# Named steps in one interleaved table, GpSimd's work moved, and a column-tiled expert gather in a one-core hybrid diffusion layer

## The chip, the cores and the metric

The kernel runs on one core of a Trainium2 chip. The metric is the device time of one execution in microseconds (us), smaller is better. Three runs of the kernel before took 646.40, 644.19 and 645.77 us; the median is 645.77.

The core has five instruction queues, each of which runs its instructions in order: TensorE (PE in the profile, its weight loads as PEld), VectorE (DVE), ScalarE (ACT), GpSimd (POOL) and SyncE (SP, which here only issues loads). An instruction that waits holds up everything behind it on its own queue.

## The reference

One trunk layer on 256 latent tokens and 256 context tokens of width 1024, in fp32. Cut to what matters:

```python
mod_x = silu(c) @ w_ada + b_ada              # six vectors of 1024: sh1, sc1, g1, sh2, sc2, g2
ux = (rms_norm(x, norm1) * (1 + sc1) + sh1) @ w_in       # and uc for the context tokens
fx, qx, kx, vx, bx, cx, hx = split_in(ux)                # kc, vc from uc
attn = na_latent(qx / 8, kx, vx, kc, vc, rpb)   # 8 heads; neighbours in the grid + all context keys, one softmax
conv = bx * short_conv(cx * hx, w_conv)         # width 3 over the positions
mixed = concat([fourier_mix(fx) @ w_fourier, attn, conv]) @ w_out
x = x + g1 * mixed
t = rms_norm(x, norm2) * (1 + sc2) + sh2
# router: best of 4 groups, then the best two of its 8 experts, softmax weights
for e in range(32):
    y += combine[:, e] * ((silu(t @ w_gate[e]) * (t @ w_up[e])) @ w_down[e])
out = rms_norm(x + g2 * y)
```

## The kernel before

**Streaming.** All large weights go through ten slabs of 16 KB per partition (2.1 MB each); an eleventh is added when the front's scratch memory is given up. `queue` fixes the order of the loads. `pump()` (L108) issues loads from SyncE while a slab is free; `drop()` (L138) gives one back. A load waits on SyncE until the last reader of the slab's old contents is done, and the loads behind it wait too. Some slabs hold no weights: `c` (context input), `g` (small operands, the convolution's data), `a` (attention bias, queries), `u`, `uh`, `ul` (the modulated input and its two exact parts), `kv`, `f` (Fourier tables), `cat` (the mixed heads).

**The front** (all before the experts) is straight-line code; its order in the source is the order on every engine. `normalise` and `transposed` bring x into feature-major form, `first_rows` and `first_columns` make the first shift and scale, `modulate` applies them, `band` (L242) makes the attention bias. `project` (L350) multiplies with both operands split in two exact parts, three products per block; `ahead` (L337) makes the parts of a weight block, the high one by ScalarE, the low one by VectorE. Order of the projections: Fourier and outer gate beside keys, then values, queries, convolution. `sums` (L308) makes the other modulation vectors on VectorE, one piece of a weight slab at a time.

**Attention** (from L460) works on two heads at a time: `scores` for both query halves (four products), bias and running minimum on VectorE, exponentials on ScalarE, division by the sum on VectorE (L481), `ptrans` transposes the probabilities, `pv` (L491) multiplies with the values. `mix` (L506) adds a row block of the output projection. GpSimd multiplies w_out by the first gate (`fold`, L501, in two calls) and does the convolution (L546 to L552). Then `x1` (L637) adds the residual, `logits` (L652) and `route` (L657) are the router.

**Experts.** Each of 32 experts has 32 places. `group(g)` (L748) gathers the tokens of four experts by products with one-hot rows, 16 products of 128 columns, and makes the weighted one-hot rows for the way back. `hidden(e)` (L785) makes the hidden layer, in four column tiles of 32; `project_down(e)` (L809) the output, and `scatter(g)` (L778) adds four experts' rows to their tokens in PSUM.

## Time and profile before

| | us |
|---|---|
| median of three runs | 645.77 |
| profiled execution, first to last instruction (span) | 641.5 |
| TensorE busy, share of the span | 476.4 (74%) |
| VectorE busy | 226.8 (35%) |
| ScalarE busy | 144.8 (23%) |
| GpSimd busy | 44.5 (7%) |
| data moved | 246.12 MB, 384 GB/s on average |
| share of DMA on the chain that ended last | 62% |

The profile is one execution. A row of a timeline reads: start, duration, engine, source line, operation, output tile, input tiles, shape and count, and in brackets how long the engine had been idle and what released it. Rows of a stage table give each engine's busy time in a stretch, the granted TensorE clock as a share of full speed, the mean busy share of the 16 DMA engines and the rate. TensorE issues a product before the one ahead has left the array, so durations overlap; start to start is the pace. Tiles have the names of the program: `b` and `m` are PSUM banks, `ws` a split weight block, `acc` the probabilities (and the partial sums before), `gu` and `dn` expert weights.

### The profile page before, as it was taken

To read this page: it belongs to the slowest core of one execution; us is meant where nothing else is said; L and a number is where in the kernel's file an instruction comes from. 1 tells how busy PE (TensorE), PEld (TensorE's weight loads), DVE (VectorE), ACT (ScalarE), POOL (GpSimd) and SP (SyncE) were. 2 spreads that over 40 slices of the span, in tenths; PEclk is the share of its full clock that TensorE was granted. 3 is DMA by queue.
4 is the path that set the end of the run, shared out by engine and by line. 5 is a ranking of instruction groups with operands and counts; after the bars stand their busy time and mean duration, and the time that the engine had idled before them with its cause. 6 is when DMAs were issued, how large, how long until landed. Compare 5 with 4: busy or idle time off the path is not lost.

```text
span 641.5 us, 11030 instructions
## 1 busy us (share of the span) xinstructions
PE 476.4 (74%) x4775; PEld 307.9 (48%) x4775; DVE 226.8 (35%) x525; ACT 144.8 (23%) x322; POOL 44.5 (7%) x44
## 2 busy tenths in 40 slices
PE   3999999887987887585567555855946585568785
PEld 3787898544775454253235222632523253235442
DVE  4767877999744222021011000211210021012323
ACT  4524234454642111011001000110100011003003
POOL 1000000894000000000000000000000000000000
PEclk9999999888997999898779778797888888789798
DMA  9999579953797999999999999999999999999992
GB/s 351 422 419 360 222 277 372 428 230 147 295 399 297 429 426 424 426 426 427 426 427 423 425 430 423 422 425 426 424 428 426 425 429 424 426 426 428 423 381 102
DMA packets 21220, 246.12 MB, mean 384 GB/s; under 512 B 2214, under 2 KB 3242, under 8 KB 6956
## 3 DMA queue, kind: packets, MB, share of 16 engines
q1 hardware_dynamic: 21016, 245.08, 91.9%
q8 instruction: 39, 0.64, 0.4%
q10 hardware_dynamic: 148, 0.27, 0.1%
q14 instruction: 17, 0.14, 0.1%
HBM read 244.28 MB, written 1.05 MB: 382 GB/s over the span
## 4 chain that ended last, share of the span: by engine, by line
DMA 62%; PE 26%; DVE 8%; ACT 1%; issue 1%; SPq 1%; DVEq 0%; ACTq 0%
DMA gu<-in_w_gu 41%; DMA dn<-in_w_dn 18%; PE b L360 11%; PE m L792 3%; DMA ada<-in_w_ada 3%; PE b L517 2%; DVE f L317 2%; DVE acc L481 2%; PE m L761 1%; PE m L814 1%; DVE ws L344 1%; PE b L261 1%; PE b L488 1%; PE m L951 1%; DVE acc L475 1%
## 5 line engine op out<-in xcount | busy, mean ns | idle before, releaser
L792 PE MATMUL m<-gu,xg 128*32 128x256 f32 x2048 | 139.9, 425 | 63.8 <-DMA gu<-in_w_gu 60.2
L792 PEld LDWEIGHTS m<-gu,xg 128*32 128x32 f32 x2048 | 72.9, 120 | 125.5 <-DMA gu<-in_w_gu 43.3
L814 PE MATMUL m<-dn,ht 128*32 128x256 f32 x992 | 74.3, 450 | 26.7 <-DMA dn<-in_w_dn 19.6
L802 DVE TENSOR_TENSOR hh<-m,sg 128x128 f32<-128x128 f32 x32 | 9.3, 291 | 182.0 <-ACT sg L800 182.0
L814 PEld LDWEIGHTS m<-dn,ht 128*32 128x32 f32 x992 | 38.8, 125 | 50.5 <-issue 38.5
L822 DVE COPY yg<-m 32x256 f32<-32x256 f32 x56 | 23.4, 418 | 99.1 <-PE m L814 86.8
L822 ACT COPY yg<-m 32x256 f32<-32x256 f32 x56 | 20.4, 364 | 142.8 <-DVE yg L822 142.8
L360 PE MATMUL b<-uh,ws 128*128 128x256 f32 (+1 forms) x224 | 52.1, 317 | 0.1
L800 ACT ACTIVATE sg<-m 128x128 f32<-128x128 f32 x32 | 8.9, 278 | 161.2 <-PE m L792 161.2
L360 PEld LDWEIGHTS b<-uh,ws 128*128 128x128 f32 x224 | 37.0, 188 | 4.7 <-issue 1.2
L360 PE MATMUL b<-ul,ws 128*128 128x256 f32 (+1 forms) x112 | 35.1, 313 | 0.0
L769 POOL TENSOR_TENSOR sw<-st,cmb 128x256 f32<-128x256 f32 x8 | 5.8, 725 | 418.4 <-DVE st L694 293.4
L783 PE MATMUL m<-yg,sl 128*128 128x512 f32 x56 | 27.7, 639 | 6.4 <-ACT yg L822 6.4
L761 PEld LDWEIGHTS m<-sr,xs 128*128 128x128 f32 x224 | 28.7, 208 | 7.7 <-PEq L887 4.8
L761 PE MATMUL m<-sr,xs 128*128 128x128 f32 x224 | 28.9, 292 | 4.0 <-DVE sr L754 4.0
L344 DVE TENSOR_TENSOR ws<-in,ws 128x1024 fp32r<-128x1024 f32 x20 | 24.4, 1221 | 14.9 <-ACT ws L343 14.8
L767 DVE TENSOR_SCALAR xg<-m,a,sh 128x128 f32<-128x128 f32 x32 | 13.1, 410 | 45.4 <-PE m L761 36.9
L804 PE MATMUL m<-ident,hh 128*128 128x128 f32 x32 | 10.9, 340 | 23.7 <-DVE hh L802 23.7
L765 ACT ACTIVATE xg<-m,sh,a 128x128 f32<-128x128 f32 x32 | 14.6, 458 | 59.4 <-DVE xg L767 59.4
L360 PE MATMUL b<-ws,uh 128*128 128x512 f32 (+1 forms) x96 | 25.9, 354 | 1.9 <-ACT uh L300 1.9
L517 PE MATMUL b<-ws,cat 128*128 128x512 f32 x96 | 24.3, 402 | 0.0
L804 PEld LDWEIGHTS m<-ident,hh 128*128 128x128 f32 x32 | 4.6, 143 | 40.9 <-DVE hh L802 40.8
(236 smaller groups left out, 574.4 us busy)
## 6 DMA issues: line engine op xcount, KB each, us to landing
gu<-in_w_gu SPq DMA_DIRECT2D x63, 2048.0 KB, 39.2
dn<-in_w_dn SPq DMA_DIRECT2D x31, 2048.0 KB, 39.1
ada<-in_w_ada SPq DMA_DIRECT2D x12, 2048.0 KB, 9.0
in<-in_w_in SPq DMA_DIRECT2D x3, 2048.0 KB, 11.3
in<-in_w_in SPq DMA_DIRECT2D x8, 512.0 KB, 17.2
out<-in_w_out SPq DMA_DIRECT2D x2, 2048.0 KB, 10.8
gu<-in_w_gu SPq DMA_DIRECT2D x4, 512.0 KB, 32.5
dn<-in_w_dn SPq DMA_DIRECT2D x3, 512.0 KB, 11.5
```

The costliest lines, as they stand in the source:

```text
L317: DVE.scalar_tensor_tensor(a, w, scx[:, j:j + 1], a, op0=OP.mult, op1=OP.add)
L344: DVE.tensor_tensor(ws[:, 1], src, ws[:, 0].bitcast(F32), OP.subtract)
L360: PE.matmul(po, wv if wst else uv, uv if wst else wv, start=(j == 0 and m == 0 and n == 0), stop=(j == NJ - 1 and m == len(parts) - 1 and ...
L517: PE.matmul(yo[t, h], cat[:, a, MIX[n], blk(t)], ws[:, b, h, :], start=(first and k == 0), stop=(last and k == 2))
L761: PE.matmul(pg[:, j, :], xs[:, t, jj * P:(jj + 1) * P], sr[:, t], start=(t == 0), stop=(t == 1))
L765: ACT.activation(xg[:, jj, :], pg[:, j, :], AF.Identity, bias=sh2[:, 0, jj:jj + 1], scale=a2[:, 0, jj:jj + 1])
L767: DVE.tensor_scalar(xg[:, jj, :], pg[:, j, :], a2[:, 0, jj:jj + 1], sh2[:, 0, jj:jj + 1], op0=OP.mult, op1=OP.add)
L783: PE.matmul(yp[2 * t + h], sl[:, t, :], yg[:, blk(h, 512)], start=(g == 0), stop=(g == NE // 4 - 2))
L792: PE.matmul(pg[32 * q:32 * q + 32], xg[:, j, CAP * i:CAP * (i + 1)], wgu[j // 4][:, :, j % 4, q * P:(q + 1) * P], start=(j == 0), stop=(j ...
L804: PE.transpose(pt, hh, ident)
L814: PE.matmul(pd[32 * q:32 * q + 32, :], ht[:, 32 * k:32 * k + 32], wdn[:, q, k, :], start=(k == 0), stop=(k == 3))
L822: (ACT.copy if q % 2 else DVE.tensor_copy)(dst, src)
```

## The change

**Named steps.** The front is cut into small functions by name; a table, `STEPS`, lists 375 of them, and they run in that order. A line of it:

```
m0t10 z3_ y3_ s4 cl0 cw1 m0t01 m4t11 hi23 s5 X4 cm1 m1t01 m4t00 cl1 E4 p1 X5 dg g3 R4 E5 lo23 e9 ph1 m2t00 S4 m2t11 pl1 m4t10 R5
```

`s5` is the pair of score products of unit 5 (two heads, one half of the queries), `X`, `E`, `R`, `S`, `t` and `y.._`/`z.._` are its bias, exponentials, division, transposes and copies, `p1` the product with the values, `m4t10` three products of row block 4 of w_out for token half 1 and output half 0, `hi`/`lo` the parts of a weight block, `e9` a piece of a sum, `d..` a slab given back.

**Work that moves.** GpSimd no longer touches w_out nor the convolution. The gate is applied by VectorE to the projected rows (`x`); the convolution is VectorE's; half of the divisions, and three of four modulations, are ScalarE's; VectorE copies half of the transposed probabilities. The load order changes, and `spare` is gone. The routing of both token halves runs after both halves' logits.

**Experts.** `group` makes only the one-hot rows; `gather(e)` gathers one expert's tokens in four column tiles and is called inside `hidden` of the expert before. The softmax weights and the rows for the way back (`weights`, `weighted`) come after the first expert's `hidden`.

```diff
-    queue += [("in", 3, w_in[3])] + first[0:2] + [("in", 2, w_in[2]), first[2], ("in", 4, w_in[4]), first[3]]
-    queue += [("small", 0, small_b)] + [("ada2", t, w_ada[8 + t]) for t in range(2)]
-    queue += [("out", 0, w_out[0])] + [("ada2", t, w_ada[8 + t]) for t in range(2, 4)] + [("out", 1, w_out[1])]
+    queue += first[0:2] + [("in", 3, w_in[3]), ("small", 0, small_b), first[2], ("in", 2, w_in[2]), first[3]]
+    queue += [("ada2", 0, w_ada[8]), ("in", 4, w_in[4]), ("ada2", 1, w_ada[9]), ("out", 0, w_out[0]), ("out", 1, w_out[1])]
+    queue += [("g2", 0, b_g2)] + [("ada2", t, w_ada[8 + t]) for t in range(2, 4)]
...
-    def fold(i):
-        for c in range(4):
-            w = loaded["out", i][:, blk(c, D)]
-            POOL.tensor_tensor(w, w, g1b, OP.mult)
...
+    @each("cw{}", range(2))
+    def _(m):
+        z = ct[:, m, :]
+        DVE.tensor_scalar(z, cp[:, m, 0:SEQ], wc[:, m:m + 1], None, op0=OP.mult)
+        for i in (1, 2):
+            DVE.scalar_tensor_tensor(z, cp[:, m, i:SEQ + i], wc[:, 2 * i + m:2 * i + m + 1], z, op0=OP.mult, op1=OP.add)
+        DVE.tensor_tensor(z, z, gbt[:, m, :], OP.mult)
...
+    @each("R{}", range(8))
+    def _(u):
+        mx, p = mxs[:, 2 * (u % 4):2 * (u % 4) + 2, :], pb[u % 2][0]
+        DVE.reciprocal(mx[:, :, 3:4], mx[:, :, 2:3])
+        DVE.tensor_scalar(p, p, mx[:, 0, 3:4], None, op0=OP.mult)
+
+    @each("S{}", range(8))
+    def _(u):
+        p = pb[u % 2][1]
+        ACT.activation(p, p, AF.Copy, scale=mxs[:, 2 * (u % 4) + 1, 3:4])
...
+    @each("x{}{}", range(2), range(2))
+    def _(t, h):
+        hs = blk(h, 512)
+        DVE.tensor_tensor(junk[:, hs], held["yo", t, h], g1b[:, hs], OP.mult)
+        DVE.tensor_tensor(xs[:, t, hs], junk[:, hs], xs[:, t, hs], OP.add)
...
+    run("g8 b0 b1 Ba0 B0 Ba1")
+    normalise(xs)
+    run("B1")
+    transposed()
+    run(STEPS)
...
+    def gather(e):
+
+        g, i = divmod(e, 4)
+        xg, sr = state[g][0], state[g][3]
+        pg = mbank((P, 256))
+        for t in range(2):
+            for q in range(4):
+                PE.matmul(pg[32 * q:32 * q + 32, :], sr[:, t, i, :], xs[:, t, blk(q, 256)], start=(t == 0), stop=(t == 1))
+        gt = mo.tile([P, 256], F32, name="gt", tag="sw")
+        (DVE.tensor_copy if e % 2 else ACT.copy)(gt, pg)
+        pt = mbank((P, 2, 4, CAP))
+        for c in range(2):
+            PE.transpose(pt[:, c], gt[:, blk(c)], ident)
+        dst = xg[:, i].rearrange("p (q c) n -> p c q n", c=2)
+        for v, op, src in ((a2, OP.mult, pt), (sh2, OP.add, dst)):
+            w = v.rearrange("p o (q c) -> p (o c) q", c=2)[..., None].to_broadcast([P, 2, 4, CAP])
+            DVE.tensor_tensor(dst, src, w, op)
...
     def expert(e):
         g, i = divmod(e, 4)
-        ht = hidden(e)
+        ht = hidden(e, {NJ - 1: (e + 1,)} if i < 3 else {}, gather)
+        if i == 0:
+            if g == 0:
+                weights()
+            weighted(g)
         project_down(e, ht, state[g][2], i)
```

TensorE's order in attention before, from the first transposes on (L488 transposes of probabilities, L467 scores, L517 output projection, L496 products with the values, L329 a sum over partitions, L596 the router's bias):

```order
L488 MATMUL b<-ident,acc 128x128 x16
L467 MATMUL b<-kv,a 128x512 x4
L517 MATMUL b<-ws,cat 128x512 x12
L496 MATMUL b<-f,kv 64x256 x8
L329 MATMUL b<-f,ones 32x256 x4
L517 MATMUL b<-ws,cat 128x512 x12
L488 MATMUL b<-ident,acc 128x128 x16
L467 MATMUL b<-kv,a 128x512 x4
L517 MATMUL b<-ws,cat 128x512 x12
L596 MATMUL b<-sa,sh_1111 1x40 x8
```

The same engine after, in the middle of attention (L699 transposes, L664 scores, L722 output projection, L709 products with the values, L470 half of the second gate):

```order
L722 MATMUL b<-ws,cat 128x512 x3
L709 MATMUL b<-f,kv 64x256 x8
L722 MATMUL b<-ws,cat 128x512 x3
L699 MATMUL b<-ident,acc 128x128 x8
L722 MATMUL b<-ws,cat 128x512 x3
L664 MATMUL b<-kv,a 128x512 x2
L722 MATMUL b<-ws,cat 128x512 x6
L664 MATMUL b<-kv,a 128x512 x2
L722 MATMUL b<-ws,cat 128x512 x6
L709 MATMUL b<-f,kv 64x256 x8
L470 MATMUL b<-ada_3_1300,scx 32x256 x16
L722 MATMUL b<-ws,cat 128x512 x9
```

Scores come two at a time instead of four, transposes eight instead of sixteen, and three to nine products of the output projection stand between them.

GpSimd's order before, from its claim of the slab `kv` on (L504 is `fold`, L548 to L552 the convolution):

```order
L92 COPY kv<-cst 128x1
L92 CAST cat<-cst 128x1
L504 TENSOR_TENSOR out_1004<-out_1004,g 128x1024 x4
L548 TENSOR_SCALAR g<-g,sa 128x256
L550 TENSOR_SCALAR g<-g,sa 128x256
L551 TENSOR_TENSOR g<-g 128x256
```

and after, from the last of its constants on (L882 is the weighted one-hot rows):

```order
L207 TENSOR_SCALAR iota_r<-iota_e 128x32
L209 TENSOR_SCALAR trib<-acc 128x128
L108 COPY kv<-cst 128x1
L108 CAST cat<-cst 128x1
L882 TENSOR_TENSOR sw<-st,cmb 128x256 x4
```

Between the claim of `cat` and the experts nothing is left on GpSimd.

TensorE's order where the experts begin, before (L761 gather, L772 transposes of the weighted rows, L792 hidden layer, L804 its transpose, L814 down product):

```order
L761 MATMUL m<-fsr,xs 128x128 x16
L772 MATMUL m<-ident,sw 128x128 x2
L792 MATMUL m<-gu_0_1153,xg 32x256 x16
L792 MATMUL m<-gu_0_1277,xg 32x256 x16
L804 MATMUL m<-ident,hh 128x128
L814 MATMUL m<-dn_1279,ht 32x256 x16
```

and after (L897 and L902 gather, L922 hidden layer, L934 its transpose, L885 the weighted rows, L944 down product):

```order
L897 MATMUL m<-xs,fsr 32x256 x8
L902 MATMUL m<-ident,gt 128x128 x2
L922 MATMUL m<-gu_0_1302,xg 32x256 x16
L922 MATMUL m<-gu_0_1412,xg 32x256 x16
L897 MATMUL m<-xs,fsr 32x256 x8
L902 MATMUL m<-ident,gt 128x128 x2
L934 MATMUL m<-ident,hh 128x128
L885 MATMUL m<-ident,sw 128x128 x2
L944 MATMUL m<-dn_1431,ht 32x256 x16
```

One expert's share of the gather stands ahead of the first expert; the next expert's share and the weighted rows stand between its hidden and its down product. (The order counts an fp32 product once; the trace shows two instructions for it.)

## Rows read from the trace of the kernel before

**Rows 1.** The page: the span, and the chain that ended last by engine.

```profile
span 641.5 us, 11030 instructions
...
DMA 62%; PE 26%; DVE 8%; ACT 1%; issue 1%; SPq 1%; DVEq 0%; ACTq 0%
```

**Rows 2.** Stage table: PE, PEld, DVE, ACT, POOL busy, clock, DMA share, GB/s.

```profile
17.20:112.40 95.20, 94.88 (x777) 80.24 (x777) 72.96 (x118) 37.69 (x60) 0.30 (x1) 1.00 0.86 344
112.40:150.00 37.60, 28.85 (x165) 18.61 (x165) 35.77 (x68) 17.54 (x39) 34.51 (x21) 0.89 0.68 280
150.00:190.80 40.80, 39.42 (x242) 28.75 (x240) 27.43 (x80) 23.38 (x50) 1.01 (x1) 0.97 0.80 317
190.80:205.60 14.80, 10.29 (x104) 8.23 (x103) 7.38 (x39) 5.41 (x13) 0.62 (x1) 0.77 0.72 282
205.60:627.00 421.40, 290.61 (x3352) 163.08 (x3352) 69.91 (x182) 47.55 (x131) 6.24 (x11) 0.88 1.00 423
```

**Rows 3.** Timeline of SyncE's load issues, 187 to 204 us.

```profile
187.38 3.84 SPq L136 DMA_DIRECT2D gu<-in_w_gu  x2
203.64 0.33 SPq L136 DMA_DIRECT2D dn<-in_w_dn  x1
```

**Rows 4.** Timeline of PE: first projection product, last logits, gather, expert 0.

```profile
17.22 0.39 PE L360 MATMUL b<-ws,uh 128*128 128x256 f32 x1 [1.92 <-ACT uh L300]
...
188.84 1.98 PE L655 MATMUL b<-sa,acc 128*128 128x40 f32 x16
...
195.49 6.00 PE L761 MATMUL m<-fsr,xs 128*128 128x128 f32 x32 [0.97 <-DVE cst L717]
...
201.65 3.66 PE L792 MATMUL m<-gu,xg 128*32 128x256 f32 x64
```

**Rows 5.** Timelines of VectorE and GpSimd: the scaling twice, the second `fold`.

```profile
141.37 2.43 DVE L481 TENSOR_SCALAR acc<-acc,mx 128x512 f32<-128x512 f32 x1
...
157.50 0.49 DVE L481 TENSOR_SCALAR acc<-acc,mx 128x512 f32<-128x512 f32 x1
...
140.94 10.07 POOL L504 TENSOR_TENSOR out<-out,g 128x1024 f32<-128x1024 f32 x4
```

**Rows 6.** Stage table, columns as above: the stretch of the small casts.

```profile
12.70:14.75 2.05, 1.90 (x65) 1.62 (x64) 1.69 (x10) 1.63 (x3) 0.00 (x0) 1.00 1.03 420
```

**Rows 7.** Groups by line, 0 to 205 us: count, busy us, mean ns.

```profile
L481 DVE TENSOR_SCALAR acc<-acc,mx 128x512 f32<-128x512 f32 x16 | 16.6, 1035 | 0.6
...
L252 DVE TENSOR_TENSOR a<-b,sa 64x192 f32<-64x192 f32 x32 | 9.8, 345 | 0.9 <-PE b L246 0.7
...
L246 PE MATMUL b<-a 96*64 96x56 bf16 x64 | 2.9, 194 | 0.0
```

**Rows 8.** Timeline of PE at the end of the projections.

```profile
112.06 0.28 PE L360 MATMUL b<-ul,ws 128*128 128x256 f32 x1
112.17 0.28 PE L360 MATMUL b<-uh,ws 128*128 128x256 f32 x1
```

**Rows 9.** Timeline of VectorE: first and last of the second half's routing.

```profile
191.75 0.25 DVE L659 SCALAR_TENSOR_TENSOR lg<-b,cst,lb 128x40 f32<-128x40 f32 x1
...
194.04 0.19 DVE L667 TENSOR_TENSOR msk<-oh 128x32 bf16<-128x32 f32 x1
```

**Rows 10.** Groups by line: to 205 us; the others from 205.6 to 627.

```profile
L559 PE MATMUL b<-ada,scx 128*32 128x256 f32 x32 | 1.9, 382 | 0.0
...
L792 PE MATMUL m<-gu,xg 128*32 128x256 f32 x1984 | 136.2, 427 | 63.8 <-DMA gu<-in_w_gu 60.2 <-ACT yg L822 3.6
...
L761 PE MATMUL m<-sr,xs 128*128 128x128 f32 x224 | 28.9, 292 | 4.0 <-DVE sr L754 4.0
```

**Rows 11.** Timeline of PE: the starts of the four score blocks.

```profile
112.38 1.99 PE L467 MATMUL b<-kv,a 64*128 64x512 f32 x8
...
128.59 1.27 PE L467 MATMUL b<-kv,a 64*128 64x512 f32 x4
...
151.08 2.56 PE L467 MATMUL b<-kv,a 64*128 64x512 f32 x8
...
162.76 2.08 PE L467 MATMUL b<-kv,a 64*128 64x512 f32 x8
```

More of the change, by code (lines that the diff above doesn't have):

```diff
@@ L2 @@
 from contextlib import ExitStack
+from functools import partial
+from itertools import product
 import numpy as np
@@ new lines, in _, with piece @@
+    @each("w{}", range(2))
+    def _(k):
+        ACT.copy(ut[:, 4:8, SEQ + k * P:SEQ + (k + 1) * P], held["ctx", k, 1])
+    def piece(kind, t, j, h, a):
+        k = 2 if kind == "ada1" else 4
+        w = loaded[kind, t].rearrange("p (j f) -> p j f", j=k)[:, j % k, blk(h, D)]
+        if j == 0:
+            DVE.tensor_scalar(a, w, scx[:, j:j + 1], None, op0=OP.mult)
+        else:
+            DVE.scalar_tensor_tensor(a, w, scx[:, j:j + 1], a, op0=OP.mult, op1=OP.add)
+        if j % k == k - 1 and (h == 1 or kind == "ada2"):
+            drop(f"{kind}_{t}")
+            pump()
@@ new lines, in tile_kernel, with _ @@
+    step["g3a"] = lambda: DVE.tensor_tensor(rg, held["g3"], rg, OP.add)
+    step["ss3"] = lambda: sum_rows("ss3", area()["acc2"])
+    step["g4"] = lambda: DVE.tensor_tensor(rg, held["ss3"], rg, OP.add)
+    @each("sp{}", range(4))
+    def _(q):
+        PE.matmul(bank((P, 256), ("sp", q)), ones[32 * q:32 * q + 1, :], area()["rg1"][32 * q:32 * q + 1, :], start=True, stop=True)
+    @each("sq1{}", range(4))
+    def _(q):
+        ACT.copy(g1b[:, blk(q, 256)], held["sp", q])
+    TERMS = ((0, 0), (0, 1), (1, 0))
@@ new lines, in tile_kernel, with _ @@
+    chunks = [("in", i, c) for c in range(4) for i in (0, 1)] + [("in", i, c) for i in (3, 2, 4) for c in range(4)] + [("out", n // 4, n % 4) for n in ORDER]
+    split, done = {}, set()
+    @each("hi{}", range(28))
+    def _(n):
+        kind, i, c = chunks[n]
+        ws = split[n] = pp.tile([P, 2, 1024], F32R, name="ws", tag="ws", bufs=3)
+        ACT.copy(ws[:, 0], loaded[kind, i][:, blk(c, 1024)])
+    @each("lo{}", range(28))
+    def _(n):
+        kind, i, c = chunks[n]
+        DVE.tensor_tensor(split[n][:, 1], loaded[kind, i][:, blk(c, 1024)], split[n][:, 0].bitcast(F32), OP.subtract)
+        done.add((kind, i, c))
+        if all((kind, i, k) in done for k in range(4)):
+            drop(f"{kind}_{i}")
+            if (kind, i) == ("in", 2):
+                held["cat"] = hold("cat", F32R).rearrange("p (s j n) -> p s j n", s=2, j=NJ)
+            pump()
@@ new lines, in keys, with keys0 @@
+    def keys(c):
+        project(1, c, [[(held["pk", m], blk(m), ALL, True)] for m in range(4)])
+    def keys0(which):
+        if which == 0:
+            for m in range(4):
+                bank((P, 512), ("pk", m))
+        project(1, 0, [[(held["pk", m][:, s], blk(m), s, True) for s in (XT, CT)] for m in range(4)], which)
+    each("k{}", range(1, 4))(keys)
+    step["kx0"], step["k0"] = partial(keys0, 0), partial(keys0, 1)
+    step["ft"] = lambda: DVE.tensor_copy(ft, held["pf"])
+    step["gb"] = lambda: ACT.copy(gbt, held["pg"])
@@ new lines, in _ @@
+    @at("kv")
+    def _():
+        drop("u")
+        kv = hold("kv")
+        held["kt"], held["vt"] = [kv[:, blk(i, 2048)].rearrange("p (m n) -> p m n", m=4) for i in range(2)]
+        pump()
+    @each("kt{}", range(4))
+    def _(m):
+        ACT.copy(held["kt"][:, m, :], held["pk", m])
+    @each("v{}", range(4))
+    def _(c):
+        if c == 0:
+            for t in range(4):
+                bank((P, 512), ("pv", t))
+        project(3, c, [[(held["pv", t], ALL, blk(t), False)] for t in range(4)])
@@ new lines, in _, with pairs @@
+    @each("vt{}", range(4))
+    def _(t):
+        ACT.copy(held["vt"][:, t, :], held["pv", t])
+    def pairs(i, key, c):
+        if c == 0:
+            for k in range(2):
+                bank((P, 2, SEQ), (key, k))
+        project(i, c, [[(held[key, k][:, m, :], blk(2 * k + m), XT, True) for m in range(2)] for k in range(2)])
+    each("q{}", range(4))(partial(pairs, 2, "pq"))
+    each("c{}", range(4))(partial(pairs, 4, "pc"))
+    step["qt0"] = lambda: ACT.copy(qt[:, 0:2, :], held["pq", 0])
@@ new lines, in tile_kernel, with mixed, _ @@
+    step["qt1"] = lambda: DVE.tensor_copy(qt[:, 2:4, :], held["pq", 1])
+    def mixed(high, j, src):
+        cat = held["cat"]
+        if high:
+            ACT.copy(cat[:, 0, j, :], src)
+        else:
+            DVE.tensor_tensor(cat[:, 1, j, :], src, cat[:, 0, j, :].bitcast(F32), OP.subtract)
+    @each("ch{}", range(2))
+    def _(s):
+        pj = bank((P, 2, 256), ("ch", s))
+        for m in range(2):
+            PE.matmul(pj[:, m, :], area()["bd"][:, s, :], area()["wf"][:, m, :], start=True, stop=True)
```

767 lines of the change are left out of this document (354 added, 413 removed).

## The prediction

> **What bounds the kernel now.** I read the page's chain first: most of the 641.5 us hangs on DMA, and the rest on TensorE [rows 1]. The stage table says where [rows 2]: from 205.6 to 627 us the DMA engines are full (share 1.00, 423 GB/s), and TensorE, busy 291 of these 421 us, waits for weights. Before 205.6 the stream has holes: shares 0.86, 0.68, 0.80, 0.72. Bytes are fixed, so the end moves only with the moment from which the stream no longer stops. SyncE's own rows show it [rows 3]: all eleven slabs hold expert weights, and the next load, a down weight, is issued at 203.64, when expert 0 has used its first slab, 2.0 us after its first product at 201.65 [rows 4]. What brings that product forward by x ends the kernel x earlier, as long as the slabs are full by then.
>
> What sets 201.65? From the first projection product at 17.22 to the last router product's end at 190.82 [rows 4] are 173.6 us, in which TensorE is busy 94.88 + 28.85 + 39.42 = 163.15 and idle 10.45, nearly all of it between 112.4 and 190.8 [rows 2]. From 112.4 to 150 VectorE is the full engine (35.77 of 37.6), and GpSimd is busy 34.51 of them. There one VectorE instruction shows two lengths: the scaling of a row of probabilities takes 2.43 us while GpSimd multiplies w_out by the gate, and 0.49 when GpSimd is idle [rows 5]. The granted clock falls to 0.89 of full there, the mean of stretches at 2.4 and at 1.2 GHz, where TensorE had idled; it was 1.00 from 17 to 112.
>
> **The change, part by part**, against the profile's 641.5 us; the runs' median, 645.77, lies 4.3 above, and I add that at the end.
>
> *Start, +2.0 (bounds 0 and +3).* VectorE now gets nine small casts (1.69 us in the stretch that holds them [rows 6]) and three band additions before the first normalisation. The additions are half as many and twice as wide: each lies between one and two of the old 0.345 us [rows 7]. That is 1.69 + 3 x 0.35..0.69 = 2.7 to 3.8, of which VectorE's wait for the inputs hides about one; the first projection product waits for this chain.
>
> *Bands, -2.5.* Seven of the eight groups of band products, 64 products in 2.9 us [rows 7], now stand ahead of the first projection, where TensorE waits.
>
> *GpSimd's work and the interleaved order, -8.0 (bounds 0 and -10.45).* Multiplying w_out and the convolution leave GpSimd; scaling the projected rows by the gate instead and the convolution cost VectorE some twelve operations of 0.4 to 0.7 us, while eight of the sixteen scalings go to ScalarE. VectorE's rows for the scalings hold 16.6 us for 16, where 16 x 0.49 = 7.8 would do: 8.8 us come back from these alone [rows 5, 7]. Part of the partial sums moves ahead of 112 us, beside the projections, where VectorE is busy 73 of 95. TensorE's products are otherwise the same ones: splitting the first key chunk into token halves makes 24 products of 512 columns into 48 of 256, and such a one is followed by the next after 0.11 us [rows 8], so nothing is added. The table puts single units (one half of the queries, two heads) and triples of output products where whole blocks stood. So I let most of the idle go and keep a quarter, 2.5 us, since VectorE stays the nearest rival. That share is a choice; the bounds are all of it kept and none.
>
> *Clock, -2.2 (bounds 0 and -4.4).* At full clock the busy time of the two late stages shrinks at most by 28.85 x 0.11 + 39.42 x 0.03 = 4.4. I take half, since waits for semaphores are counted in it.
>
> *Router, +0.7 (bounds 0 and +2).* The two token halves' routing, of which the first now runs beside the second's products, stands wholly behind the last product: 18 operations. Twelve of this kind take 191.75 to 194.23, 0.207 each [rows 9]: 3.7 us, then 0.3 for the rank products and 7 x 0.207 = 1.4 for the placing, 5.4 against 195.49 - 190.82 = 4.7 now [rows 4].
>
> *First gather, -2.8 (bounds -1.5 and -4).* Now 32 instructions and their evictions stand between 195.49 and expert 0's 201.65: 6.2 us [rows 4]. After it is one expert's share: 16 instructions in tiles of 32 columns, half of a row of 32 with 1.9 us [rows 10], so 1.0; then a copy, two transposes, two VectorE operations of about 0.4 and the hand-offs, 2.4. The softmax weights and the slots' transposes move behind expert 0's first products. They hold up its down product by some sixteen operations of 0.207, 3.3 us, and with it that slab; but the two slabs freed before it give the stream work for 9.9 us (2.1 MB at 423 GB/s are 4.96). In the later groups 28.9 us for 28 experts is 1.03 each [rows 10], what the new form costs too. The two extra transposes and evictions of each expert, some 1 us, fall into waits for gate and up weights (60.2 us [rows 10]); without that cover they would be 28 us.
>
> Sum: +2.0 - 2.5 - 8.0 - 2.2 + 0.7 - 2.8 = -12.8. Expert 0 starts at 188.9, the stream is unbroken from there, the span is 628.7, and with the 4.3 that lie around it the time is **633.0**.
>
> **Two rules of the Trainium skill.** Rows first: beside GpSimd's multiply the scaling takes 2.43 us, alone 0.49 [rows 5]. [...] And: the last projection product is followed by the first score product after 0.21 us instead of 0.11 [rows 8, 11]. "TensorEngine Tiling (Array Packing)" (Key Properties) says that a change of tiling mode drains TensorE; four more score blocks are eight more changes, 0.8 us against the change. By it the sum would be -12.0 instead of -12.8.
>
> **Rivals.**
> *The stream, not expert 0, decides: 627.* By the new queue only the last convolution chunks free slabs for the second half of the second gate and for the experts. With scores from about 102 (below) and the Fourier products after them, the conv chunks run from about 107 to 122; loads then wait until about 115 and again to 124 and 137. From there ten slabs of 4.96 us last to 187; issued loads start about 2 us after their row, so today's counterpart is 205.6. No early expert 0 gains more than 18.6: 627.2. For: the holes of today. Against: expert 0 would have to start before 183, which takes no idle and the full clock.
> *The idle stays: 643.* If handing over unit by unit makes TensorE wait as often in small pieces as now in large ones, and the clock falls as now, the terms are +2.0 - 2.5 + 0.7 - 2.8 = -2.6: 643.2. For: TensorE runs in order, and one late unit holds up everything behind it. Against: 11.7 us for the pair of scores after GpSimd is done, with the products between them [rows 11].
> *The units go through too slowly: 648.7, slower.* Four accumulators of the output projection hold half of the eight PSUM banks, and scores, transposes and products with the values must share four. Today the starts of the score blocks lie 16.2 and 22.5 us apart beside GpSimd, 11.7 after it [rows 11]. If the mean of the first two, 19.35, is the chain's own pace and not GpSimd's, four pairs take 77.4, and 16.4 follow (190.8 - 162.8 less a pair of 11.7). Scores start at about 102 (112.4, less 96 products x 0.115 that now come later, plus the start): logits end at 195.8, 5 later than now. With router and gather, 201.65 + 5 + 0.7 - 2.8 = 204.5: 2.9 slower, 648.7. Slower than now it is from 18.6 us a pair on.
>
> **How the numbers follow.** Forecast 0.57 (628 to 639), stream 0.16, idle 0.18, slow units 0.07, anything else 0.02. A difference under 0.3%, 1.9 us, cannot be told here from none. The idle rival lies on that border, so a third of it goes to "same". Faster 0.57 + 0.16 + 0.12 = 0.85, same 0.07, slower 0.08. For the likeliest alone the bounds give -2.5 + (0 to 3) + (0 to -10.45) + (0 to -4.4) + (0 to 2) + (-1.5 to -4), which I do not expect to fall on one side together: 626 to 643. Seen with the rivals, the range that leaves out no more than two in ten is 623 to 645: it takes in the idle rival with half of what a run varies, and the stream rival.
>
> **What would show it.** Right: expert 0's first product at 185 to 194, the next down load 2 us after it, and a full stream from there; GpSimd idle between 112 and the experts, scalings at 0.5 us throughout; TensorE over 95% busy from the first projection to the router, at clock 1.00; first projection product near 19; 5 to 6 us from the last router product to the first gather, 3 to 4 from there to expert 0. Wrong: long waits of TensorE on VectorE or ScalarE between scores and transposes (idle or slow rival); the stream empty while TensorE runs on and expert 0 before 183 (stream); or holes in the stream behind expert 0, which would mean that the late down product or the new gathers hold slabs.

## The result, and the profile after

The changed kernel takes 641.11 us (median of 8 runs, 640.13 to 643.3), the kernel before 645.3 (8 runs, 643.36 to 646.4): ratio 0.9947, 95% interval 0.993 to 0.9964. Forecast was 633.0. The sign and the range (623 to 645) held; of the 12.8 us forecast, 4 came. Medians here and below are those of the undisturbed executions: a single one, 737.18 us in the run with the router's pauses filled, is left out.

The two profiles are one execution each. The one after is the slowest of its eight (643.3 us, span 641.4); a span of 641.5 before goes with a time of 643.38 in later runs of the same kernel, which is its fast end. So the spans differ by 0.1 us where the medians differ by 4.2: of the losses read from this pair below, some 4 us would then be the spread between executions.

First the page, span and chain, against [rows 1]. DMA no longer holds most of the chain; TensorE does:

```profile
span 641.4 us, 11767 instructions
...
PE 46%; DMA 43%; DVE 7%; ACT 2%; issue 2%; POOL 0%; DVEq 0%; ACTq 0%; POOLq 0%; SPq 0%
```

The stage table after, columns as in [rows 2]:

```profile
20.70:112.40 91.70, 91.06 (x701) 74.76 (x702) 67.56 (x100) 43.50 (x78) 2.35 (x2) 1.00 0.85 341
112.40:150.00 37.60, 37.60 (x272) 27.71 (x270) 32.08 (x80) 22.74 (x47) 0.00 (x0) 1.00 0.74 279
150.00:180.00 30.00, 29.83 (x192) 21.34 (x191) 19.62 (x48) 15.39 (x33) 0.00 (x0) 1.00 0.96 390
180.00:205.60 25.60, 15.49 (x145) 6.89 (x147) 7.82 (x46) 4.35 (x10) 0.61 (x1) 0.64 0.89 366
205.60:620.00 414.40, 289.60 (x3562) 148.32 (x3555) 88.44 (x225) 40.38 (x116) 5.55 (x11) 0.90 1.00 421
```

From the first projection product to 180 us TensorE is idle 0.8 us (0.64 + 0 + 0.17) instead of 10.45, at full clock. The scalings left to VectorE last 0.49 us each, where [rows 5, 7] had 2.43 and a mean of 1.035. Groups by line, 95 to 180 us:

```profile
L687 DVE TENSOR_SCALAR acc<-acc,mx 128x512 f32<-128x512 f32 x8 | 3.9, 487 | 0.3
```

The timeline of TensorE from the last logits on, against [rows 4]:

```profile
177.16 2.87 PE L778 MATMUL b<-sa,x1t 128*128 128x40 f32 x24
182.22 0.19 PE L829 MATMUL b<-msk,trib 128*128 128x32 bf16 x1 [2.19 <-DVE msk L796]
...
183.71 1.94 PE L897 MATMUL m<-xs,fsr 128*32 128x256 f32 x16 [1.12 <-DVE cst L836]
...
187.85 6.56 PE L922 MATMUL m<-gu,xg 128*32 128x256 f32 x64 [0.98 <-DVE xg L906]
194.24 1.04 PE L897 MATMUL m<-xs,fsr 128*32 128x256 f32 x16
...
197.52 0.33 PE L934 MATMUL m<-ident,hh 128*128 128x128 f32 x1 [1.18 <-DVE hh L932]
201.33 0.69 PE L885 MATMUL m<-ident,sw 128*128 128x128 f32 x2 [3.48 <-POOL sw L882]
201.95 3.64 PE L944 MATMUL m<-dn,ht 128*32 128x256 f32 x32
205.36 4.66 PE L922 MATMUL m<-gu,xg 128*32 128x256 f32 x64
```

Expert 0 starts at 187.85 instead of 201.65: 13.8 us earlier, 1 more than forecast. But its 64 gate and up products take 6.56 us, not 3.66, and its down product comes 14.1 us behind its first product. Before, at full clock and with the slots (the weighted one-hot rows for the way back) ready, that distance was 5.1, 201.65 to this row:

```profile
206.74 1.93 PE L814 MATMUL m<-dn,ht 128*32 128x256 f32 x32 [0.38 <-DVE ht L806]
```

The stage table after has the clock of that stretch, at half of full or little above it:

```profile
183.70:187.85 4.15, 2.63 (x19) 0.90 (x19) 0.91 (x3) 1.66 (x2) 0.00 (x0) 0.50 1.02 432
187.85:194.40 6.55, 6.55 (x68) 3.12 (x72) 0.28 (x1) 0.00 (x0) 0.00 (x0) 0.55 0.93 358
```

SyncE's issues show what this does to the stream. Those after, against [rows 3]:

```profile
176.45 3.98 SPq L152 DMA_DIRECT2D gu<-in_w_gu  x2
191.55 0.33 SPq L152 DMA_DIRECT2D dn<-in_w_dn  x1
194.48 11.49 SPq L152 DMA_DIRECT2D gu<-in_w_gu  x2
208.36 0.33 SPq L152 DMA_DIRECT2D dn<-in_w_dn  x1
```

The first slab is free at 191.55, the second at 194.48, and the third, expert 0's down weights, only when the pair's second load is issued, at the end of its row, 205.97. Before, the first was free at 203.64 [rows 3], and the row of the next pair ends at 209.07:

```profile
205.37 3.70 SPq L136 DMA_DIRECT2D gu<-in_w_gu  x2
```

After, the DMA engines stand seven tenths empty for 4 us (stretches, columns as above):

```profile
0.00:90.00 90.00, 77.75 (x700) 67.78 (x704) 66.33 (x108) 40.85 (x74) 2.97 (x11) 1.00 0.98 394
90.00:130.00 40.00, 40.00 (x282) 30.61 (x277) 28.03 (x66) 25.12 (x49) 1.17 (x1) 1.00 0.42 149
130.00:188.00 58.00, 53.01 (x351) 35.01 (x351) 42.62 (x123) 27.01 (x55) 0.00 (x0) 0.93 0.98 395
188.00:202.00 14.00, 8.71 (x89) 3.90 (x89) 3.33 (x16) 2.33 (x7) 0.61 (x1) 0.74 0.98 399
202.00:206.00 4.00, 4.00 (x41) 1.89 (x44) 0.35 (x1) 0.37 (x1) 0.00 (x0) 0.50 0.29 123
```

The same stretches before, up to 188 us:

```profile
0.00:90.00 90.00, 78.11 (x677) 65.83 (x677) 62.61 (x127) 37.89 (x65) 2.11 (x11) 1.00 0.90 361
90.00:130.00 40.00, 37.14 (x282) 29.38 (x280) 35.15 (x51) 15.07 (x28) 15.11 (x8) 0.96 0.86 350
130.00:188.00 58.00, 50.79 (x284) 35.15 (x284) 44.91 (x111) 31.66 (x65) 20.41 (x14) 0.94 0.65 256
```

Rate times length gives 64.3 MB moved by 188 us after and 61.3 before: the stream is 3.0 MB ahead there, 7 us at 425 GB/s.

At the far end, expert 27's down product is the last work of TensorE that waits for a weight. Before (first of the two views) it starts at 568.83 and expert 28 at 580.71, 11.9 us behind it:

```profile
568.83 3.54 PE L814 MATMUL m<-dn,ht 128*32 128x256 f32 x32 [1.95 <-DMA dn<-in_w_dn]
573.29 3.70 PE L783 MATMUL m<-yg,sl 128*128 128x512 f32 x8 [0.93 <-ACT yg L822]
576.83 3.73 PE L761 MATMUL m<-sr,xs 128*128 128x128 f32 x32
...
580.71 3.66 PE L792 MATMUL m<-gu,xg 128*32 128x256 f32 x64
```

After, it is 17.2 us, since four gathers stand one behind the other (two of the four are shown):

```profile
562.88 3.37 PE L944 MATMUL m<-dn,ht 128*32 128x256 f32 x32 [2.20 <-DMA dn<-in_w_dn]
567.17 3.70 PE L913 MATMUL m<-yg,sl 128*128 128x512 f32 x8 [0.93 <-ACT yg L952]
570.80 1.07 PE L897 MATMUL m<-xs,sr 128*32 128x256 f32 x16
572.37 0.44 PE L902 MATMUL m<-ident,gt 128*128 128x128 f32 x2 [0.49 <-ACT gt L899]
...
578.07 1.07 PE L897 MATMUL m<-xs,sr 128*32 128x256 f32 x16
579.75 0.44 PE L902 MATMUL m<-ident,gt 128*128 128x128 f32 x2 [0.62 <-DVE gt L899]
580.12 3.66 PE L922 MATMUL m<-gu,xg 128*32 128x256 f32 x64
```

From expert 28's first product both kernels need 61 us to the end (641.5 - 580.71, 641.4 - 580.12). So 13.8 us at expert 0 are 5.95 at expert 27 and 0.6 at expert 28. The experiments ask where the 7.9 and the 5.35 went.

### The profile page after: what moved, and what is told of

Same layout as the page of the kernel before. It is cut to its first block, busy times and chain, and to the rows that moved or that the text cites. A ratio compares the mean times of both kernels' runs of the same rounds, so it can differ in the third digit from the quotient of the medians.

```text
span 641.4 us, 11767 instructions
## 1 busy us (share of the span) xinstructions
PE 486.1 (76%) x5133; PEld 294.5 (46%) x5133; DVE 234.8 (37%) x552; ACT 142.2 (22%) x319; POOL 10.3 (2%) x24
## 4 chain that ended last, share of the span: by engine, by line
PE 46%; DMA 43%; DVE 7%; ACT 2%; issue 2%; POOL 0%; DVEq 0%; ACTq 0%; POOLq 0%; SPq 0%
DMA gu<-in_w_gu 24%; DMA dn<-in_w_dn 18%; PE b L524 12%; PE m L922 8%; PE m L944 5%; PE b L722 4%; PE m L897 2%; PE m L913 2%; PE b L664 1%; PE b L709 1%; DVE xg L906 1%; PE b L699 1%; DVE a L293 1%; PE b L310 1%; PE m L902 1%
## 5 line engine op out<-in xcount | busy, mean ns | idle before, releaser
L922 PE MATMUL m<-gu,xg 128*32 128x256 f32 x2048 | 132.1, 409 | 39.9 <-DMA gu<-in_w_gu 33.0
L922 PEld LDWEIGHTS m<-gu,xg 128*32 128x32 f32 x2048 | 70.8, 118 | 97.5 <-DMA gu<-in_w_gu 35.9
L944 PE MATMUL m<-dn,ht 128*32 128x256 f32 x992 | 82.3, 489 | 16.0 <-DMA dn<-in_w_dn 7.3
L944 PEld LDWEIGHTS m<-dn,ht 128*32 128x32 f32 x992 | 38.4, 136 | 47.8 <-issue 32.0
L906 DVE TENSOR_TENSOR xg<-m,a 128x256 f32<-128x256 f32 x32 | 13.6, 425 | 83.0 <-PE m L902 83.0
L524 PEld LDWEIGHTS b<-uh,ws 128*128 128x128 f32 x240 | 39.1, 188 | 4.8 <-issue 2.8
L934 PE MATMUL m<-ident,hh 128*128 128x128 f32 x32 | 10.1, 314 | 35.1 <-DVE hh L932 35.1
L899 DVE COPY gt<-m 128x256 f32<-128x256 f32 x16 | 6.8, 425 | 78.8 <-PE m L897 78.8
L897 PE MATMUL m<-xs,sr 128*32 128x256 f32 x448 | 31.7, 402 | 4.5 <-PEq L1024 4.5
L902 PE MATMUL m<-ident,gt 128*128 128x128 f32 x64 | 14.3, 307 | 19.0 <-DVE gt L899 10.8
L495 ACT CAST ws<-in 128x1024 fp32r<-128x1024 f32 x20 | 21.0, 1049 | 33.2 <-PE b L524 30.7
L722 PE MATMUL b<-ws,cat 128*128 128x512 f32 x96 | 27.4, 414 | 0.0
L934 PEld LDWEIGHTS m<-ident,hh 128*128 128x128 f32 x32 | 4.5, 140 | 45.2 <-issue 28.8
## 6 DMA issues: line engine op xcount, KB each, us to landing
dn<-in_w_dn SPq DMA_DIRECT2D x3, 512.0 KB, 11.5
```

The lines of the kernel that those rows point to most:

```text
L495: ACT.copy(ws[:, 0], loaded[kind, i][:, blk(c, 1024)])
L524: PE.matmul(po, st, mv, start=begins, stop=(c == 3 and tail and not any(po is v[1] for v in todo[n + 1:])))
L722: PE.matmul(held["yo", t, h], held["cat"][:, a, MIX[n], blk(t)], ws[:, b, h, :], start=(held["nm", t, h] == 0), stop=(held["nm", t, h] == ...
L897: PE.matmul(pg[32 * q:32 * q + 32, :], sr[:, t, i, :], xs[:, t, blk(q, 256)], start=(t == 0), stop=(t == 1))
L902: PE.transpose(pt[:, c], gt[:, blk(c)], ident)
L906: DVE.tensor_tensor(dst, src, w, op)
```

## The experiments

Each was timed beside the kernel before on the same chip; ratios are to that, with a 95% interval in brackets. Four chips were used (runs one to four, five to eight, nine to twelve, and the last two), on which the kernel before took 645.38, 644.40, 645.36 and 645.18 us; so between these sets a difference of medians is uncertain by about 1 us, and the ratio counts. The first four edit the changed kernel, the next four the version of the first of them; after these, each says what it edits.

**The last group at once.** In the last group the gather of before (`gather_all`, 32 products and eight evictions; its body is not shown):

```
-            gather(e + 1)
+            gather_all(g + 1) if e == NE - 5 else gather(e + 1)
...
-    for i in (1, 2, 3):
-        gather(NE - 4 + i)
```

> The changed kernel, but the last group's gather is done at once, in 32 products of 128 columns with eight evictions, as in the kernel before; the other groups keep the column-tiled gather per expert. Theory (the four column-tiled gathers of the last group stand one behind the other in front of its first expert, and from that expert on nothing waits for the stream, so each of their microseconds ends the kernel later): from the down product of expert 27 to the first product of expert 28 it takes 11.9 us as before, not 17.2; time 641.1 - 5.3 = 635.8. Rival (the stream sets the end, so the tail only waits less elsewhere): expert 28 then waits for its gate and up weights, time within 0.3% of 641.1.

It takes 635.86 us, a ratio of 0.9858 (0.9841 to 0.9876), where the changed kernel has 0.9947 (0.993 to 0.9964). From the down product (561.57) to expert 28 (575.58) it took 14.0 us in the profiled execution, where the group's scatter took 5.73 us instead of 3.70 (granted clock 0.65 from 566 to 572), and 12 with that difference off. The theory holds: the tail's 5.3 us are shown.

**The weights behind expert 0's down product.**

```
-        if i == 0:
-            if g == 0:
-                weights()
+        if i == 0 and g:
             weighted(g)
         project_down(e, ht, state[g][2], i)
+        if e == 0:
+            weights()
+            weighted(0)
```

> The changed kernel, but the softmax weights and the weighted slots of the first group stand behind expert 0's down product instead of in front of it. Theory (the down product of expert 0 is held 3.5 us by that chain, its slab comes free as much later, and the stream has a hole of some 3.5 us at 202 to 206): down product at about 198.3 instead of 201.95, the hole gone, stream and kernel 3.5 us earlier: 637.6. Rival (the holes at 90 to 130 us alone set where the stream stands): the down product is earlier, the stream's last load is issued at the same time as now, 597.9, time within 0.3% of 641.1.

It takes 643.24 us, 0.9984 (0.9968 to 1.0): a miss, and slower than the changed kernel. The timeline of TensorE shows why: the down product is at 197.27, as expected, but the slots' transposes now hold up expert 1, which starts at 206.69 (205.36 in the changed kernel):

```profile
197.27 2.73 PE L944 MATMUL m<-dn,ht 128*32 128x256 f32 x32 [0.38 <-DVE ht L936]
206.08 0.69 PE L885 MATMUL m<-ident,sw 128*128 128x128 f32 x2 [6.08 <-POOL sw L882]
206.69 6.21 PE L922 MATMUL m<-gu,xg 128*32 128x256 f32 x64
```

TensorE works in order: the wait was moved by one expert, not removed.

**Products that keep the clock.** Nine products of `xs` by the identity, of 512 columns and with a result that nobody reads, in TensorE's pauses of the router and of the first gather.

> The changed kernel with nine products of 512 columns more, whose result nobody reads, in TensorE's pauses of the router and of the first gather. Theory (after these pauses the clock stands at half, so expert 0's gate and up products take 6.56 us instead of 3.7): granted clock near 1.00 at 184 to 192, these products 3.7 us, expert 0's first slab free 1 to 2 us earlier and its down product 3 us earlier, time 641.1 - 2.9 = 638.2. Rival (the slabs were not full yet when expert 0 began, so its pace costs the stream nothing): time within 0.3% of 641.1.

It takes 642.51 us, 0.9959 (0.9942 to 0.9975): no gain. The clock was 1.00 from 180 to 195, and expert 0's products took 3.66 us. But the first four products were too many: they put off the rank products by 1.8 us and expert 0 to 190.19, and the down product still waited for the slots, 3.48 us, and stood at 201.37.

**All three.**

> All three together: last group's gather at once, first group's weights behind expert 0's down product, products that keep the clock up. Theory: the two front edits take away the same hole, of which 3.9 us is all there is (0.07 x 6.5 + 0.71 x 4 + 0.05 x 12 us of idle DMA time behind expert 0's start), and the tail gives its 5.3 besides: 641.1 - 3.9 - 5.3 = 631.9. Rival for the front (holes at 90 to 130 alone): 635.8. Rival for the tail (the stream sets the end): 637 to 638.

The three edits together take 635.85 us, 0.9858 (0.9844 to 0.9872): as with the last group at once alone ("the tail alone" below). The front pair gave nothing, since the second edit's wait stayed: no product ran from 200 to 205.

**The weights spread over experts 1 and 2.**

```
         project_down(e, ht, state[g][2], i)
+        if e == 1:
+            weights()
+        if e == 2:
+            weighted(0)
```

> The changed kernel with the last group's gather at once (this and the next three runs are held against that version, 635.86), and the first group's softmax weights moved to behind expert 1's down product, its weighted slots behind expert 2's, where nobody waits for them. Before this, putting both behind expert 0's down product only moved TensorE's wait of 6.1 us to in front of expert 1. Theory (TensorE's in-order queue, held by the slots' transposes, is what leaves the stream with a hole behind expert 0): no wait of over 2 us for the slots, expert 0's down product near 197, DMA share 0.97 or more from 200 to 215, expert 27's down product 2 us earlier, time 633.9. Rival (the holes at 90 to 130 us have put the stream so far back that experts 0 to 3 cost it nothing): 635.9 within 0.3%.

It takes 634.46 us, 0.9841 (0.9826 to 0.9856), 1.4 less than the tail alone by the medians; the intervals overlap. Expert 0's down product is at 197.31, the DMA share at 202 to 206 is 1.01 (0.67 with the tail alone, 0.29 in the changed kernel), and expert 27's down product is at 559.91, 1.7 earlier:

```profile
188.00:202.00 14.00, 11.54 (x139) 5.74 (x143) 3.15 (x9) 1.01 (x3) 0.00 (x0) 0.75 0.95 372
202.00:206.00 4.00, 3.45 (x64) 1.89 (x54) 0.00 (x0) 0.55 (x2) 0.00 (x0) 1.00 1.01 430
```

**Two loads more.**

```
+                if kind == "gu0" and i in (1, 2):
+                    again = ("gu0", 0) if i == 1 else ("gu1", 0)
+                    SP.dma_start(loaded[again], (w_gu[0, 0], w_gu[0, 1])[i - 1])
                 SP.dma_start(loaded[kind, i], src)
```

> The last group's gather at once, and two loads more: both gate and up slabs of expert 0 are loaded a second time over themselves, behind the loads of expert 0 and of the next slab, long before they are used. That is 4.2 MB, 9.9 us of the stream. Theory (from 130 us on the stream runs without a break up to expert 0, so it and not expert 0's start is what the later loads wait for): only the hole behind expert 0 (2 to 4 us) can take some of it up, so 635.9 + 6 to 8 = 642 to 644. Rival (expert 0's start and pace hold the stream, as the forecast had it, and slabs are full when it begins): the loads go into slack, 635.9 to 638.

It takes 639.55 us, 0.9928 (0.9914 to 0.9943): 3.7 more, between theory and rival. The DMA share is 1.00, 1.01 and 1.01 from 130 to 188, to 202 and to 206, where it was 0.98, 0.97 and 0.67: by shares the holes there took up 3 of the 9.9 us (0.02 x 58 + 0.04 x 14 + 0.34 x 4). By rates it is more: 415, 428 and 430 GB/s instead of 392, 389 and 238 are 2.6 MB, 6 us. Expert 27's down product is 3.8 us later, which also leaves 6 taken up: from 130 us on the stream had no more than that to give away.

**The first group at once too.** The softmax weights ahead of expert 0, beside its gather, as before:

```
     group(0)
-    gather(0)
+    weights()
     onehot(0, fst)
+    gather_all(0)
+    weighted(0)
```

> The last group's gather at once, and the first group's gather at once too, with its softmax weights beside it and its slots ahead of expert 0, as in the kernel before. The forecast's step (one expert's gather first is worth 2.8 us at the start and so at the end): expert 0 at 189.9 to 190.7 instead of 188, time 635.9 + 2.8 = 638.7. Theory (what counts is when slabs come free behind expert 0, not when it begins): with full clock and the weights ready its down product comes at about 195 instead of 201, the hole is gone, time 634 to 636.

It takes 633.13 us, 0.9843 (0.9819 to 0.9868). Expert 0 starts 2.4 us later than with the tail alone, and yet expert 27's down product is at 559.35, 2.2 earlier. The timeline of TensorE:

```profile
183.68 6.62 PE L915 MATMUL m<-fsr,xs 128*128 128x128 f32 x32 [1.12 <-DVE cst L836]
190.14 0.38 PE L885 MATMUL m<-ident,sw 128*128 128x128 f32 x2
190.45 3.66 PE L938 MATMUL m<-gu,xg 128*32 128x256 f32 x64
194.83 0.33 PE L950 MATMUL m<-ident,hh 128*128 128x128 f32 x1 [0.72 <-DVE hh L948]
195.54 1.93 PE L960 MATMUL m<-dn,ht 128*32 128x256 f32 x32 [0.38 <-DVE ht L952]
197.30 3.64 PE L938 MATMUL m<-gu,xg 128*32 128x256 f32 x64
```

The gather at once is itself 6.6 us of products; the granted clock is 0.50 in its first half and 1.00 when expert 0's products run, and the weights get ready beside it. Expert 1 then follows expert 0 in 6.85 us, not in 17.5 as in the changed kernel. Against the tail alone it is 2.7 us by the medians, which are of two chips, and 1.0 by the ratios (0.9858 and 0.9843), whose intervals overlap: this run alone does not settle the gain. Two runs below keep this edit and add others that should cost nothing (every group at once, the router's pauses filled). They lie at 633.38 and 633.06 us with ratios of 0.9819 and 0.9818, 2.5 us below the tail alone; their intervals end at 0.9842 and 0.984, where that of the tail alone begins (0.9841).

**The start later.** `normalise` and `transposed` ahead of the casts and bands.

> The last group's gather at once, and the nine casts and the first band additions stand behind the first normalisation and its transposes instead of ahead of them. For the start term: the first projection product comes 1.5 to 3.5 us earlier than the changed kernel's 20.7, and expert 0 as much earlier than 188 (if nothing in between takes it up). By the forecast the time follows, 635.9 - 2.5 = 633.4; by the theory that the stream's holes at 90 to 130 decide, it follows only as far as slabs come free earlier there: 633.4 to 635.9.

It takes 638.41 us, 0.991 (0.9894 to 0.9926), 2.5 slower than the tail alone, a miss: the products that make the first shift and scale stand behind the bands' in TensorE's queue, so the first projection product came at 22.88, not earlier. The casts' place ahead of the normalisation is right. Why the start costs 3.5 us instead of 2.0, the timelines of the two kernels show: the transposes of x start 1.4 later (10.71, before 9.29), behind the band additions on VectorE; the products for the first shift and scale start 1.6 later still (15.70, before 12.64), since 24 band products now stand ahead of them; and from there to the first projection product it takes 0.45 more.

**Every group at once.** An edit of the version with first and last group at once: `gather_all` and `weighted` for each.

> The changed front with the gather of the kernel before in every group (the version with the first and the last group at once, 633.13, is what this and the next two are held against). The forecast costed the new form in the later groups at nothing, under waits for weights. If that holds and the old form hides as well: 633.1 within 0.3%. If the four serial experts' transposes and evictions cost the stream something in the middle groups, this is 1 to 3 us faster; if the 32 products in one piece make the stream wait at each group's end, it is 1 to 3 us slower.

It takes 633.38 us, 0.9819 (0.9796 to 0.9842), the same as 633.13 within the noise: in the middle groups both forms hide, as forecast.

**GpSimd back.** In that version, eight multiplies of w_out by a column of ones, written behind the score steps s1 and s2.

> First and last group at once, and GpSimd multiplies w_out again, eight multiplies of 128 x 1024 as in the kernel before but by one, behind the second and third score blocks; VectorE keeps its new work, so only the multiply beside it comes back. Theory (the multiply holds up VectorE's scalings, and TensorE waits for those): some scalings at 2.4 us again instead of 0.49, TensorE idle 3 to 8 us between 115 and 150, clock under 1.00 there, expert 0 at 193.5 to 198.5 instead of 190.5, time 636 to 641. Rival (the interleaved order, not GpSimd, is what keeps TensorE fed; the scalings have slack): expert 0 within 1 us of 190.5, time 633.1 within 0.3%.

It takes 634.49 us, 0.9839 (0.9820 to 0.9859); expert 0 starts at 190.69. It does not tell the theories apart: w_out had landed early and GpSimd ran ahead, from 95 to 114 us, so that one scaling alone met it (2.13 us).

**The kernel before without its multiply.** `fold` does nothing, so the gate of the attention's output is left out of the result.

> The kernel before without its eight multiplies of w_out by the gate on GpSimd; the gate of the attention's output is left out of the result. The order and all else stay. Theory (GpSimd's multiply alone makes most of the idle between 112 and 150): scalings near 0.5 us, TensorE's idle between 112 and 190 down from 10 us to 4 or less, expert 0 at 195 to 198 instead of 201.65, time 645.0 - 4 to 6 = 639 to 641. Rival (the order makes the idle; GpSimd's work only stretches what has slack): expert 0 within 1.5 us of 201.65, time 643.5 to 645.

It takes 632.15 us, 0.981 (0.9788 to 0.9832), 13 us faster than before, twice what was expected: expert 0 starts at 190.72. From 112.4 us to the last router product TensorE is idle 4.3 us instead of 10.1, and busy 64.0 instead of 68.3, now at a granted clock of 1.00. The groups by line show what the multiply had cost VectorE: the scalings 8.4 us of 16.6, [rows 7], and others beside it:

```profile
L317 DVE SCALAR_TENSOR_TENSOR f<-ada,scx,f 128x1024 f32<-128x1024 f32 x10 | 13.5, 1350 | 0.2
L344 DVE TENSOR_TENSOR ws<-out,ws 128x1024 fp32r<-128x1024 f32 x8 | 9.6, 1217 | 0.4 <-ACT ws L343 0.4
...
L481 DVE TENSOR_SCALAR acc<-acc,mx 128x512 f32<-128x512 f32 x16 | 8.2, 510 | 0.6
```

The first two took 15.5 (mean 1545 ns) and 11.1 (1402) in the kernel before.

**The router's pauses filled.** Three products of 512 columns whose result nobody reads, in the version with first and last group at once.

> First and last group at once, and three products of 512 columns, whose result nobody reads, in TensorE's two pauses of the router. The first group's gather takes 6.6 us there at half clock. If the pauses are filled, clock 1.00 at 183 to 190, the gather 3.7 to 4.5 us, expert 0 at 188 to 188.5 instead of 190.45, and as the stream has a hole of 1.3 us between 188 and 200, the time is 1 to 1.3 us less: 632. Rival (evictions set the gather's end, or the stream does not wait for expert 0): 633.1 within 0.3%.

It takes 633.06 us, 0.9818 (0.9795 to 0.984): the gather took 3.81 us at a clock of 1.00, expert 0 started at 188.08, and the time is the same within the noise. In the profiled execution expert 27's down product is at 557.29, 2.1 earlier than with first and last group at once (559.35). So the stream did get further; that the 2.4 us did not come out in the time is not explained.

What was still open after these twelve was which part of the largest term makes the front's gain, the multiply taken away or the new order; the last two runs went there.

**One part alone: the gate on the rows, in the old order.**

```
-            POOL.tensor_tensor(w, w, g1b, OP.mult)
...
-            DVE.tensor_tensor(xs[:, t, hs], yo[t, h], xs[:, t, hs], OP.add)
+            DVE.tensor_tensor(junk[:, t, hs], yo[t, h], g1r[:, hs], OP.mult)
+            DVE.tensor_tensor(xs[:, t, hs], junk[:, t, hs], xs[:, t, hs], OP.add)
```

> The kernel before with one part of the change alone: GpSimd's multiply of w_out is gone and the gate is put on the projected rows instead (four operations of VectorE more, 128 x 512, at 0.7 us each, of which two pairs stand on the path in front of the router). Order, convolution on GpSimd and gathers as before. Theory (GpSimd's multiply beside the scalings is what costs the front): 632.2, the time without any gate, plus 1.4 to 2.8: 633.5 to 635, expert 0 near 192. Rival (the new order earns its part): 637 or more.

It takes 638.63 us, 0.9899 (0.9882 to 0.9915), on the rival's side. Expert 0 starts at 195.73: 6 of the 11 us that it gained without any gate. The gate's four multiplies, each with its addition, stand in the old order right ahead of the router (170.64 to 173.38, 179.74 to 182.47), with TensorE waiting behind them; the difference to the run without a gate is 5 us.

**GpSimd tied to the score blocks, in the new order.** An edit of the version with first and last group at once.

> The changed kernel with first and last group at once (633.13), and GpSimd's eight multiplies of 128 x 1024 by one back, each four tied to a value that the score blocks' first reductions give, so that they run beside the scalings. Theory: scalings beside them at 2.4 us, TensorE idle 3 us or more between 112 and 150, time 636 to 641. Rival (the new order has so much slack that even there the multiply costs little): idle under 1.5 us, time within 0.3% of 633.1, or 634.5 as where the multiply ran earlier.

It takes 636.43 us, 0.9875 (0.9849 to 0.9901). The multiplies ran from 108 to 116 and from 119 to 128 us and met three of the eight scalings, which took up to 1.93 us (mean of all 772 ns). TensorE is idle 1.1 us from 112 to 150, and expert 0 starts at 191.59, 1.1 later:

```profile
112.40:150.00 37.60, 36.48 (x265) 27.19 (x263) 35.63 (x76) 22.90 (x47) 12.36 (x7) 1.00 0.66 249
```

The time lies in the theory's range, the idle in the rival's, and the runs spread from 634.06 to 639.87. In the new order the multiply costs some 3 us (against 633.1 to 633.4), in the old one 13; part of that is that it meets fewer scalings there.

## Why the prediction was wrong

By its own terms, forecast and measured up to expert 0:

| term | forecast | measured | from |
|---|---|---|---|
| start | +2.0 | +3.5 | first projection product 20.73, before 17.22 |
| work, the idle kept | -8.0 | -9.6 | idle 10.45 to 0.8 |
| bands and clock | -4.7 | -4.7 | busy 163.15 to 158.49 (91.06 + 37.60 + 29.83) |
| router | +0.7 | -1.0 | 183.71 - 180.03, before 4.7 |
| first gather | -2.8 | -2.0 | 187.85 - 183.71, before 6.16 |
| sum | -12.8 | -13.8 | 201.65 to 187.85 |

The front was right as a sum, and in part by luck: the large terms came near their size, but the start cost 1.5 more than forecast and the router 1.7 less, both outside their bounds. The router was over-charged: the routing that was put at 3.7 us took 2.2 (VectorE, 180.07 to 182.29), the two halves' operations lying closer than 0.207 us apart.

Two steps behind it failed. The first is "expert 0 starts at 188.9, the stream is unbroken from there", with its ground that two slabs give the stream work for 9.9 us while the late down product costs 3.3. From the first slab's release to the third's it was 14.4 us (191.55 to 205.97), 5.4 before: the slots' wait was 3.5, as costed, but two terms were left out. One is the clock: TensorE had been idle 3.3 of the 3.7 us ahead of the gather, and at 0.50 to 0.55 of full clock expert 0's products cost 2.9 us more and the down product 1.7 more. The other is expert 1's gather, which stands between expert 0's hidden and down product and was put at nothing: 3.1 us from the last gate and up product to the transpose of the hidden layer (194.41 to 197.52), 0.7 before. Of 13.8 us 5.95 arrived at expert 27.

How much of expert 0's lead over the kernel before arrives at expert 27's down product, the runs show side by side (one execution each; the changed kernel and the tail alone have the same code up to there):

| run | expert 0 earlier by | expert 27 earlier by |
|---|---|---|
| changed kernel | 13.8 | 5.95 |
| tail alone | 13.6 | 7.3 |
| weights spread | 13.4 | 8.9 |
| router's pauses filled | 13.6 | 11.5 |
| every group at once | 12.5 | 10.2 |
| first and last group at once | 11.2 | 9.5 |
| gate on the rows, old order | 5.9 | 5.7 |
| no multiply, old order | 10.9 | 11.05 |

With the first group's gather at once some 2 us are lost, with one expert's gather first 4.4 to 8 (so too in the runs that are not listed); the tail alone and the filled pauses have the same start of expert 0, 188.06 and 188.08. Undoing that step, with an expert 0 that starts later, wins 1.0 us (by its ratio) to 2.7 us (by its median). The edit forecast at -2.8 is worth +1 to +2.7: the start of expert 0 was taken for the gain, where the release of its slabs is. It is also not true that slabs were full by then: the hole at 90 to 130 us (share 0.42, before 0.86) had moved there, so that the stream was only 7 us ahead at 188, and the two extra loads show that 6 us of slack were left. That this moved hole makes the 2 us which are lost even with the first group at once is likely, as the two runs in the old order do not lose them, but no run here changes it alone.

The second is a step that was not made: the tail was carried over unchanged. The cover named for the extra transposes, waits for gate and up weights, holds in the middle groups, as the run with every group at once shows. It does not exist in front of expert 28, where four experts' gathers stand in a row with 61 us behind them that wait for no weight: 5.3 us, shown by the first run.

By the medians 2.7 and 5.3 are the 8 us between forecast and result: with both undone the kernel takes 633.1 to 633.4, ratios of 0.9843 to 0.9818 where the forecast was 0.980. That this meets 633.0 is in part luck, since expert 0 then starts at 190.45 and not at 188.9. The 4.3 us that the sum set between span and time are 1.9 in every run (641.4 and 643.3, 641.5 and 643.38); the other 2.4 are that the profiled execution before was faster than the median. They cancel in the difference.

Of the rivals none came true as told. The stream rival was right in part, since its holes moved to 90 to 130 and its later part had little slack, but it needed an expert 0 before 183. The idle rival and the slow units are out: 0.8 us idle. Of the large term, 6 us come with the move of the gate from GpSimd to the rows in the old order; the 5 that the gate on the rows costs there are hidden by the new order, which is argued from the difference of two runs.

## What to carry to other kernels

An earlier start is worth what it brings forward the release of what the bottleneck waits for: time the third buffer's release, not the first product. When one form of a step replaces another everywhere, cost it at the first and the last place apart, where the cover of the steady loop is missing. A piece of work that lets the clock return and others get ready may be worth its own length.

## What was not expected of the hardware

After TensorE had been idle 3.3 of 3.7 us in the router, the same 64 products of expert 0 took 6.56, 6.55, 5.27, 5.22, 5.21 and 5.04 us in six executions with the same code ahead of them or nearly so, and 3.66 where nine more products stood in the pauses. Without GpSimd's eight multiplies (21.5 us of its own time), and without any gate, the kernel before is 13 us faster, more than the 8.4 that the scalings lose. And 2.4 us of earlier expert 0 with nothing behind it late (188.08 instead of 190.45) changed the time by nothing that can be measured, although expert 27's down product came 2.1 earlier.
